# Three edits of an encoder kernel: where VectorE and GpSimd add, where the meta column is summed, and split weights kept in DRAM

## The chip, the cores and the metric

One Trainium2 chip, of which the kernel uses one core. A core has TensorE (PE, with its weight loads shown apart as PEld), VectorE (DVE), ScalarE (ACT), GpSimd (POOL) and SyncE (SP), which here issues every DMA. The metric is the device time of one execution, in microseconds; three runs of the kernel before are taken and their median counts. A further run is profiled.

## What is computed

One layer of a bidirectional encoder on two sequences with shared weights, one of 1024 tokens (s = 0, the long one) and one of 512 (s = 1, the sample). Sixteen meta tokens stand in front of each and are dropped at the end. Everything is float32.

```python
def mixer_sublayer(x, ...):
    n = rms_norm(x, g_mix)
    qa, ka, va, qb, kb, vb = jnp.split(n @ w_in, cuts, axis=-1)
    ...
    return x + concat(oa, ob) @ w_out

def conv_glu_sublayer(x, ...):
    n = rms_norm(x, g_ffn)
    gate = n @ w_ff_gate
    pad = jnp.pad(gate, ((0, 0), (1, 1), (0, 0)))
    gate = pad[:, :-2] * conv_w[0] + pad[:, 1:-1] * conv_w[1] + pad[:, 2:] * conv_w[2] + conv_b
    return x + (gelu(gate) * (n @ w_ff_up)) @ w_ff_down
```

After it comes a last RMSNorm. The model width is 1024, the feed-forward width 2816 (22 tiles of 128). The convolution looks one token to each side, so the first real token needs the gate of the last meta token: this one extra column is the meta column of the text.

## The kernel before

**Float32 products.** Activations lie with the features on the partitions and the tokens along the free dimension. Each operand of a product is split into a rounded part and a rest: `split` (L101) copies to `hi` on ACT (L104) and subtracts to `lo` on DVE (L105). `mm3` (L108) then multiplies three times, hi by hi, hi by lo and lo by hi (L110 to L112), into one PSUM sum. So each weight tile costs an ACT copy and a DVE subtraction before PE may use it. `split_half` (L129) splits 512 columns into one of five `w_hi` and one of five `w_lo` buffers (HB = 5).

**Order.** The program is scheduled as a whole ahead of the run: a scheduler orders the instructions of each engine by program order and its own idea of when they are ready. On the chip each engine then goes through its list in order, SP too, so an instruction that waits holds up all behind it on its engine.

**Stages.** The projections and attentions of both sequences come first and fill more than half of the time. The sample's `mixer_out` (L524, from about 519 us) runs beside the long sequence's attention; it loads each w_out tile, splits it and uses it (`load_weight`, L149, with three buffers each). The sample's `conv_glu` follows. The part that the change touches is mainly what comes after the long attention:

- `mixer_out_long` (L566, about 1345 to 1487 us) computes x + mix @ w_out for the long sequence in three parts of the tokens (PARTS). For each part it goes over the eight w_out tiles j anew: `load_halves` (L142) loads the tile and splits both halves, 24 matmuls follow, DVE adds the residual (L652), SP stores the sum `h`, and ACT and POOL sum squares. When a part is done, `combine` (L580) normalises it and splits the combinations that the next stage multiplies; it is a generator whose steps are taken between the tiles of the next part.
- `conv_glu_long` (L830, about 1487 to 2002 us) goes over eleven pairs of feed-forward tiles. A pair takes two fast products in Winograd's form (`winograd`, L785), one for the gate and one for w_up: seven products of half-size blocks instead of eight. Within one, the weight sums s1 to s4 are made on POOL (L794), the products land in one of eight PSUM buffers, and the sums of products are formed in `u` and `v` (ACT copies at L812 and L816, additions through L807 on DVE and, for `v`, on POOL). The meta column is a product with one column: ACT scales the raw weights by the column (L860), DVE reduces over the eight blocks (L862), PE sums over the partitions with a matrix of ones (L864), and ACT puts the result into the gate (L865). Then follow the convolution (L871 on ACT, L872 and L874 on DVE) and the GELU (L876). For w_up, DVE adds the product to the rest (L884) and POOL multiplies it by the gate's GELU (L885). POOL forms the activation differences for the down product (L893), and SP stores all seven operands in DRAM.
- The down product (from L904, about 2002 to 2258 us) is again such a fast product, seven products q = 0 to 6 over eleven steps f; the last one is cut in two halves. Here the weights' blocks a11 to a22 are loaded once and kept, `operand` (L938) forms the sums on POOL in place, `split_act` splits the activations, which are loaded for each product, and after each product four PSUM tiles are added to `u`, `v`, `c11`, `c22` on DVE (L997). The residual is added by POOL (L967). `norm` writes the output.

`load` (L919) keeps its DMAs in one fixed order. All of them stand on SP's queue.

## Time and profile before

| What | us |
|---|---|
| median of three runs | 2265.46 (2263.97 to 2266.13) |
| profiled execution | 2260.37 |
| its span, first to last instruction | 2258.6 |

The mean granted clock of TensorE is 0.963 of full speed. In the profile, a group of instructions is a line of the kernel, an engine, an operation and the tiles out<-in with their shape; then the count, the busy time in us, the mean of one in ns, and the idle time of that engine just before them with what ended most of it. Buffer numbers are left out of names, so `w_f` stands for `w_f` and `w_f2`. A table by windows gives, for each stretch, the busy time of each engine with the count of its instructions, the granted clock, the busy share of the 16 DMA engines and what they moved. Matmuls overlap each other, so the duration of one is longer than the step from one to the next.

### The profile page before, as it was taken

To read this page: it belongs to the slowest core of one execution; us is meant where nothing else is said; L and a number is where in the kernel's file an instruction comes from. 1 tells how busy PE (TensorE), PEld (TensorE's weight loads), DVE (VectorE), ACT (ScalarE), POOL (GpSimd) and SP (SyncE) were. 2 spreads that over 40 slices of the span, in tenths; PEclk is the share of its full clock that TensorE was granted. 3 is DMA by queue.
4 is the path that set the end of the run, shared out by engine and by line. 5 is a ranking of instruction groups with operands and counts; after the bars stand their busy time and mean duration, and the time that the engine had idled before them with its cause. 6 is when DMAs were issued, how large, how long until landed. Compare 5 with 4: busy or idle time off the path is not lost.

```text
span 2258.6 us, 35389 instructions
## 1 busy us (share of the span) xinstructions
PE 2075.1 (92%) x12186; PEld 1838.7 (81%) x12186; DVE 1708.6 (76%) x3599; ACT 1229.1 (54%) x2325; POOL 1140.6 (50%) x832
## 2 busy tenths in 40 slices
PE   7898998997999999999998999678999899998897
PEld 6898888996978998998998989676777777776677
DVE  6877787758788678888879766797767776747796
ACT  6534566635566565677667655455434444434354
POOL 3466456764454333455444313245566557526852
PEclk8999999998999999999999999888999999999999
DMA  6555334446312222232332237622222222265234
GB/s 222 165 183 184 114 108 145 157 167 195 101 59 66 96 71 75 81 113 90 104 101 72 75 102 212 175 74 87 93 84 103 80 84 101 86 212 184 80 119 134
DMA packets 156452, 268.52 MB, mean 119 GB/s; under 512 B 19792, under 2 KB 88944, under 8 KB 155760
## 3 DMA queue, kind: packets, MB, share of 16 engines
q1 hardware_dynamic: 156272, 266.26, 36.6%
q8 instruction: 96, 1.57, 0.3%
q14 instruction: 84, 0.69, 0.1%
HBM read 193.31 MB, written 72.88 MB: 118 GB/s over the span
## 4 chain that ended last, share of the span: by engine, by line
PE 53%; DVE 20%; issue 8%; POOL 7%; ACT 6%; DMA 5%; SPq 1%; POOLq 0%; DVEq 0%; ACTq 0%
PE ps_mm L111 12%; PE ps_mm L110 12%; PE ps_mm L112 12%; DVE w_lo L105 5%; PE ps_t L398 5%; PE ps_s L375 3%; PE ps_s L376 3%; DVE p L377 2%; DVE acc L862 2%; ACT w_hi L104 1%; PE ps_o L413 1%; PE ps_o L412 1%; DMA w_f<-w_out 1%; POOL act L885 1%; DVE act L872 1%
## 5 line engine op out<-in xcount | busy, mean ns | idle before, releaser
L110 PE MATMUL ps_mm<-xhi,w_hi 128*128 128x258 f32 (+3 forms) x1264 | 389.3, 308 | 12.1 <-ACT xhi L205 7.1
L111 PE MATMUL ps_mm<-xlo,w_hi 128*128 128x258 f32 (+3 forms) x1264 | 382.1, 302 | 9.2 <-DVE xlo L105 4.3
L112 PE MATMUL ps_mm<-xhi,w_lo 128*128 128x258 f32 (+3 forms) x1264 | 380.4, 301 | 0.0
L105 DVE TENSOR_TENSOR w_lo<-w_f,w_hi 128x512 fp32r<-128x512 f32 (+1 forms) x216 | 275.4, 1286 | 92.4 <-ACT w_hi L104 91.9
L377 DVE TENSOR_SCALAR_CACHE_REDUCE p<-ps_s 114x344 f32<-114x344 f32 (+4 forms) x562 | 257.7, 487 | 38.8 <-PE ps_s L376 20.8
L382 ACT ACTIVATE p<-p,nm 114x1040 f32<-114x1040 f32 (+5 forms) x212 | 215.0, 1014 | 87.3 <-DVE nm L380 83.9
L110 PEld LDWEIGHTS ps_mm<-xhi,w_hi 128*128 128x128 f32 x1264 | 241.6, 191 | 18.9 <-ACT xhi L205 8.0
L111 PEld LDWEIGHTS ps_mm<-xlo,w_hi 128*128 128x128 f32 x1264 | 241.9, 191 | 15.0 <-DVE xlo L105 5.4
L449 POOL TENSOR_TENSOR p<-p,r 128x1040 f32<-128x1040 f32 (+1 forms) x96 | 159.2, 1665 | 185.0 <-DVE r L384 115.8
L104 ACT CAST pt_hi<-ps_t 128x512 fp32r<-128x512 f32 (+6 forms) x360 | 168.4, 482 | 147.3 <-PE ps_t L398 127.0
L104 ACT CAST w_hi<-w_f 128x512 fp32r<-128x512 f32 (+1 forms) x233 | 187.0, 818 | 103.2 <-PE ps_mm L111 50.9
L112 PEld LDWEIGHTS ps_mm<-xhi,w_lo 128*128 128x128 f32 x1264 | 241.6, 191 | 0.9
L105 DVE TENSOR_TENSOR pt_lo<-ps_t,pt_hi 128x512 fp32r<-128x512 f32 (+4 forms) x312 | 171.9, 561 | 46.6 <-ACT pt_hi L104 45.2
L375 PE MATMUL ps_s<-k,q 128*114 128x348 f32 (+4 forms) x552 | 183.9, 338 | 14.5 <-DVE p L377 13.8
L398 PE MATMUL ps_t<-ident,p 128*128 128x128 f32 (+7 forms) x1188 | 184.1, 271 | 3.3 <-DVE pt_lo L105 2.1
L104 ACT CAST w_hi<-w_s 128x512 fp32r<-128x512 f32 x114 | 70.5, 619 | 208.3 <-PE ps_mm L111 113.1
L471 POOL TENSOR_TENSOR p<-p,c 114x1040 f32<-114x1040 f32 (+2 forms) x56 | 92.2, 1646 | 178.5 <-DVE c L469 111.4
L376 PE MATMUL ps_s<-k,q 128*114 128x348 f32 (+4 forms) x552 | 172.6, 317 | 0.4 <-DMA q<-qk 0.4
L398 PEld LDWEIGHTS ps_t<-ident,p 128*128 128x128 f32 (+7 forms) x1188 | 141.2, 136 | 33.2 <-issue 6.6
L110 PE MATMUL ps_s<-xhi,w_hi 128*128 128x256 f32 (+4 forms) x480 | 147.4, 312 | 10.6 <-ACT xhi L205 7.9
L112 PE MATMUL ps_s<-xhi,w_lo 128*128 128x256 f32 (+4 forms) x480 | 146.9, 307 | 4.4 <-DVE w_lo L105 4.3
L111 PE MATMUL ps_s<-xlo,w_hi 128*128 128x256 f32 (+4 forms) x480 | 147.2, 308 | 1.1 <-DVE xlo L105 1.0
(257 smaller groups left out, 5851.5 us busy)
## 6 DMA issues: line engine op xcount, KB each, us to landing
w_f<-w_gate SPq DMA_DIRECT2D x44, 512.0 KB, 3.3
w_f<-w_up SPq DMA_DIRECT2D x44, 512.0 KB, 3.3
w_f<-w_in SPq DMA_DIRECT2D x36, 512.0 KB, 4.0
w_f<-w_out SPq DMA_DIRECT2D x32, 512.0 KB, 4.2
a_f<-act SPq DMA_DIRECT2D x64, 256.0 KB, 2.7
w_f<-w_down SPq DMA_DIRECT2D x22, 512.0 KB, 3.3
act<-a_t SPq DMA_DIRECT2D x44, 256.0 KB, 2.0
a<-w_down SPq DMA_DIRECT2D x42, 256.0 KB, 3.8
```

The source lines that it names most:

```text
L104: nc.scalar.copy(hi, src)
L105: (lo_engine or nc.vector).tensor_tensor(out=lo, in0=src, in1=hi.bitcast(F32), op=ALU.subtract)
L110: nc.tensor.matmul(ps, lhsT=whi, rhs=xhi, start=start, stop=False)
L111: nc.tensor.matmul(ps, lhsT=whi, rhs=xlo, start=False, stop=False)
L112: nc.tensor.matmul(ps, lhsT=wlo, rhs=xhi, start=False, stop=stop)
L375: nc.tensor.matmul(ps, lhsT=q[0], rhs=k[:, c0:c0 + cw], start=True, stop=False)
L376: nc.tensor.matmul(ps, lhsT=q[1], rhs=k[:, c0:c0 + cw], start=False, stop=True)
L377: nc.vector.tensor_scalar(out=p[:, c0:c0 + cw], in0=ps, scalar1=HD ** -0.5, scalar2=-3.0e38, op0=ALU.mult, op1=ALU.max, accum_out=mx[:, i: ...
L382: nc.scalar.activation(p, p, AF.Exp, bias=nm, accum_out=l)
L398: nc.tensor.transpose(tps[:, c:c + M], p[:, k0:k0 + kw], g.ident[:M, :M])
L449: nc.gpsimd.tensor_tensor(out=p, in0=p, in1=r.broadcast_to([P, n]), op=ALU.mult)
L471: nc.gpsimd.tensor_tensor(out=p1, in0=p1, in1=c.broadcast_to([M, n]), op=ALU.mult)
```

## The change

There are three edits.

**VectorE in place of GpSimd.** In `winograd` the product p5 stays in PSUM and `v` is formed as p5 + u on DVE, where ACT had copied it and POOL had added. For w_up, DVE adds in PSUM and multiplies by the gate, where POOL had multiplied. In the down product the sums of weights move to DVE. Two of them are formed earlier: s2 during product 1 and a12 - a11 during product 2. For that, a21 is loaded for each step of product 0 and a22 for each step of product 1. The residual is loaded ahead into four buffers and added on DVE in PSUM; the one for `u` stays on POOL, after product 3.

**The meta column.** The scaled copies and the reductions are written at the head of a pair, before the gate's products; the matmuls with the ones stay behind these.

**Split parts in DRAM.** The sample's `mixer_out` stores the two parts of six w_out tiles (`PRE`), and `mixer_out_long` loads these parts, each in halves, where it had loaded and split the tile. Halves are now taken with the second one first.

```diff
...
 def load_halves(g, wp, src):
 
     w = load_whole(wp, g, src)
-    parts = [split_half(g, wp, w[:, i * H:(i + 1) * H]) for i in range(2)]
+    parts = [split_half(g, wp, w[:, i * H:(i + 1) * H]) for i in (1, 0)][::-1]
     return [p[0] for p in parts], [p[1] for p in parts]
+def load_parts(g, wp, src):
+    out = [None] * 2, [None] * 2
+    for i in (1, 0):
+        for part, tl, tag in zip(src, out, ("w_hi", "w_lo")):
+            tl[i] = wp.tile([P, H], F32R, name=tag, tag=tag, bufs=HB)
+            g.nc.sync.dma_start(out=tl[i].bitcast(F32), in_=part[:, i * H:(i + 1) * H])
+    return out
 
 
 def load_weight(g, wp, src, bufs=2, ahead=2, lo_engine=None):
...
                 split(g, xhi[k][:, c0:c0 + cw], xlo[k][:, c0:c0 + cw], m)
         for j in range(KT):
             w = load_weight(g, wp, g.w_out[j], bufs=wb)
+            if j in PRE:
+                for part, tl in zip(g.wo[j], w):
+                    nc.sync.dma_start(out=part, in_=tl.bitcast(F32))
             for c0, cw in chunks:
                 real = min(cw, C - 1 - c0)
                 res = mp.tile([P, cm], F32, name="res", tag="m")[:, :cw]
...
                 rows = g.oT[0][k * P:(k + 1) * P]
                 split(g, xhi[k], xlo[k], loaded("m", MB, rows[:, 1:], rows[:, 0:1]))
             for j in range(KT):
-                wj = load_halves(g, wp, g.w_out[j])
+                wj = load_parts(g, wp, g.wo[j]) if j in PRE else load_halves(g, wp, g.w_out[j])
                 rows = g.xT[0][j * P:(j + 1) * P]
                 res = loaded("res", 2, rows[:, NMETA:], rows[:, NMETA - 1:NMETA])
                 ps = g.psum.tile(P, cw, "s")
...
     def tile(tag):
         return up.tile([P, H], F32, name=tag, tag=tag, bufs=2)[:, :cw]
 
-    def add(engine, out, a, b):
-        engine.tensor_tensor(out=out, in0=a, in1=b, op=ALU.add)
+    def add(out, a, b):
+        nc.vector.tensor_tensor(out=out, in0=a, in1=b, op=ALU.add)
 
     s1 = s_(ALU.add, a21, a22)
     p1 = product(split_half(g, wp, a11), x["x11"])
...
     nc.scalar.copy(u, p1)
     yield 0, 0, product(split_half(g, wp, a12), x["x21"]), u
     p5 = product(split_half(g, wp, s1), x["t1"])
-    v = tile("v")
-    nc.scalar.copy(v, p5)
     s2 = s_(ALU.subtract, s1, a11)
     p6 = product(split_half(g, wp, s2), x["t2"])
-    add(nc.vector, u, p6, u)
-    add(nc.gpsimd, v, u, v)
+    add(u, p6, u)
+    v = tile("v")
+    add(v, p5, u)
     s3 = s_(ALU.subtract, a11, a21)
     p7 = product(split_half(g, wp, s3), x["t3"])
-    add(nc.vector, u, p7, u)
+    add(u, p7, u)
     yield 1, 1, p7, v
     s4 = s_(ALU.subtract, a12, s2)
     yield 0, 1, product(split_half(g, wp, s4), x["x22"]), v
...
     for f0 in range(0, NFF, 2):
         gate = up.tile([P, 2, N + 1], F32, name="gate", tag="gate", bufs=1)
         raw = [load_whole(wp, g, g.w_gate[f0 + i]) for i in range(2)]
+        first_sums = []
+        for i in range(2):
+            prod = up.tile([P, KT, P], F32, name="prod", tag="prod", bufs=1)
+            for k in range(KT):
+                nc.scalar.activation(prod[:, k], raw[i][:, k * P:(k + 1) * P], AF.Copy, scale=g.x0[:, k:k + 1])
+            acc = up.tile([P, P], F32, name="acc", tag="acc")
+            nc.vector.tensor_reduce(out=acc, in_=prod.rearrange("p k c -> p c k"), axis=AX.X, op=ALU.add)
+            first_sums.append(acc)
 
         for c0, cw in ((0, first), (first, H - first)) if f0 == 0 else ((0, H),):
             for i, half, ps, rest in winograd(g, wp, up, x, raw, c0, cw):
...
             es_h.close()
             ap = pool(es, g, "fa0", 1, "left")
         act = ap.tile([P, 2, N], F32, name="act", tag="act", bufs=2)
         for i in range(2):
-            prod = ap.tile([P, KT, P], F32, name="prod", tag="prod")
-            for k in range(KT):
-                nc.scalar.activation(prod[:, k], raw[i][:, k * P:(k + 1) * P], AF.Copy, scale=g.x0[:, k:k + 1])
-            acc = ap.tile([P, P], F32, name="acc", tag="acc")
-            nc.vector.tensor_reduce(out=acc, in_=prod.rearrange("p k c -> p c k"), axis=AX.X, op=ALU.add)
             ps = g.psum.tile(P, 2, "mm")
-            nc.tensor.matmul(ps, lhsT=acc, rhs=g.ones_d[:, 0:2], start=True, stop=True)
+            nc.tensor.matmul(ps, lhsT=first_sums[i], rhs=g.ones_d[:, 0:2], start=True, stop=True)
             nc.scalar.activation(gate[:, i, 0:1], ps[:, 0:1], AF.Copy, scale=float(D))
         for i in range(2):
             f = f0 + i
...
         raw = [load_whole(up, g, g.w_up[f0 + i], "w_f2") for i in range(2)]
         for i, half, ps, rest in winograd(g, wp, up, x, raw, 0, H):
             a = act[:, i, half * H:(half + 1) * H]
-            t = ap.tile([P, H], F32, name="sum", tag="sum", bufs=2)
-            nc.vector.tensor_tensor(out=t, in0=ps, in1=rest, op=ALU.add)
-            nc.gpsimd.tensor_tensor(out=a, in0=t, in1=a, op=ALU.mult)
+            nc.vector.tensor_tensor(out=ps, in0=ps, in1=rest, op=ALU.add)
+            nc.vector.tensor_tensor(out=a, in0=ps, in1=a, op=ALU.mult)
         (x11, x12), (x21, x22) = [[act[:, i, half * H:(half + 1) * H] for half in range(2)] for i in range(2)]
 
         def kept_act(nm, src):
...
         return blocks[nm, f]
 
     def sum_(out, op_, a, b):
-        nc.gpsimd.tensor_tensor(out=out, in0=a, in1=b, op=op_)
+        nc.vector.tensor_tensor(out=out, in0=a, in1=b, op=op_)
         return out
 
     def stage():
...
     def operand(q, f):
         if q < 2:
             w = weight(("a11", "a12")[q], f)
-            if f % 2 == q:
-                weight("a21", f)
+            weight(("a21", "a22")[q], f)
+            if q == 1:
+                sum_(blocks["a11", f], ALU.subtract, sum_(stage(), ALU.add, blocks["a21", f], blocks["a22", f]),
+                     blocks["a11", f])
             return w
         a11, a12, a21, a22 = [weight(nm, f) for nm in ("a11", "a12", "a21", "a22")]
         if q == 2:
 
-            return sum_(a11, ALU.subtract, sum_(stage(), ALU.add, a21, a22), a11)
+            sum_(a12, ALU.subtract, a12, a11)
+            return a11
         if q == 3:
-            sum_(a12, ALU.subtract, a12, a11)
             return sum_(stage(), ALU.add, a21, a22)
         if q == 4:
 
...
 
     u, v, c11, c22 = [result(nm) for nm in ("u", "v", "c11", "c22")]
 
-    def residual(out, k0, half):
+    def residual(k0, half):
+        out = []
         for j in range(HT):
-            res = op.tile([P, H], F32, name="res", tag="res", bufs=2)
-            nc.sync.dma_start(out=res, in_=g.h[k0 + j, :, half * H:(half + 1) * H])
-            nc.gpsimd.tensor_tensor(out=out[:, j], in0=out[:, j], in1=res, op=ALU.add)
+            out.append(op.tile([P, H], F32, name="res", tag="res", bufs=4))
+            load(out[j], g.h[k0 + j, :, half * H:(half + 1) * H])
+        return out
 
     def square(src, cw):
         sq = op.tile([P, H], F32, name="sq", tag="sq", bufs=4)[:, :cw]
...
             if f == LAGF and waiting:
                 waiting()
                 waiting = None
+            if f == LAGF and q in (1, 3, 4, 5):
+                res = residual(*{1: (0, 0), 3: (HT, 0), 4: (HT, 1), 5: (0, 1)}[q])
         cc = slice(c0, c0 + cw)
         for j in range(HT):
+            def out(tl, rest):
+                plus(ps[j], ps[j], rest)
+                plus(tl, ps[j], res[j])
             if q == 0:
                 nc.scalar.copy(u[:, j], ps[j])
             elif q == 1:
-                plus(c11[:, j], ps[j], u[:, j])
+                out(c11[:, j], u[:, j])
             elif q == 3:
                 plus(v[:, j], ps[j], u[:, j])
+            elif q == 4:
+                plus(u[:, j], ps[j], u[:, j])
+                out(c22[:, j], v[:, j])
             elif q == 5:
-                plus(v[:, j], ps[j], v[:, j])
+                out(v[:, j], v[:, j])
             else:
-                if q == 4:
-                    plus(c22[:, j], ps[j], v[:, j])
                 plus(u[:, j, cc], ps[j], u[:, j, cc])
+            if q == 3:
+                nc.gpsimd.tensor_tensor(out=u[:, j], in0=u[:, j], in1=res[j], op=ALU.add)
         if q == 1:
-            residual(c11, 0, 0)
             squares(acc1, c11, True)
         elif q == 4:
-            residual(c22, HT, 1)
-            residual(v, 0, 1)
-            residual(u, HT, 0)
             squares(acc2, c22, True)
         elif q == 5:
             squares(acc2, v, False)
...
 K2 = 8
 MB = 3
 HB = 5
+PRE = (0, 1, 2, 4, 5, 6)
 SB = 2
 AT = 3
 AF_ = 4
...
+    g.wo = {j: dram.tile([2, P, D], F32, name=f"wo{j}") for j in PRE}
     g.act = dram.tile([NFF // 2, len(TS), P, H], F32, name="act0")
     nc.scalar.preload_act_table_set(EXP_LN)
     g.vec = const.tile([P, V_N], F32, name="vec")
```

## The prediction

> **What bounds the kernel now.** I read the page first, for the busy shares, then the clock of each stretch in a table by windows, then, stage by stage, the matmul groups with the idle time before them, and last the timeline around one such gap.
>
> ```profile
> span 2258.6 us, 35389 instructions
> PE 2075.1 (92%) x12186; PEld 1838.7 (81%) x12186; DVE 1708.6 (76%) x3599; ACT 1229.1 (54%) x2325; POOL 1140.6 (50%) x832
> ...
> PE 53%; DVE 20%; issue 8%; POOL 7%; ACT 6%; DMA 5%; SPq 1%; POOLq 0%; DVEq 0%; ACTq 0%
> ```
>
> PE is busy 92% of the span. So a change to the other engines pays only where PE stands still, or where its clock is reduced.
>
> ```profile
> 520.00:530.00 10.00, 4.85 (x18) 3.26 (x18) 5.26 (x18) 6.38 (x11) 4.52 (x4) 0.70 0.98 335
> 1360.00:1450.00 90.00, 80.70 (x495) 76.65 (x493) 62.35 (x116) 45.23 (x99) 30.07 (x32) 0.96 0.78 222
> 1440.00:1486.00 46.00, 28.38 (x162) 26.30 (x160) 37.51 (x57) 23.10 (x40) 8.80 (x8) 0.85 0.49 141
> 1486.00:1534.00 48.00, 32.78 (x173) 30.30 (x173) 42.98 (x55) 24.78 (x52) 20.68 (x14) 0.76 0.15 47
> 1574.00:1976.00 402.00, 374.18 (x1557) 300.43 (x1555) 288.78 (x292) 177.64 (x355) 249.55 (x163) 0.96 0.26 89
> 1706.00:1750.00 44.00, 41.52 (x181) 33.39 (x179) 31.74 (x33) 19.28 (x39) 27.43 (x19) 1.00 0.26 90
> 2002.00:2036.00 34.00, 29.10 (x117) 23.86 (x118) 14.88 (x22) 15.35 (x27) 0.23 (x1) 0.90 0.91 321
> 2067.00:2110.00 43.00, 29.92 (x103) 21.71 (x103) 28.84 (x23) 11.74 (x21) 43.00 (x29) 0.84 0.35 110
> ```
>
> Columns: stretch, length, busy time of PE, PEld, DVE, ACT, POOL, granted clock, DMA share, GB/s. The rows are: the sample's output projection starting; the long sequence's output projection (parts 0 and 1, then part 2); the first pair of feed-forward tiles; nine later pairs; one pair alone; the start of the down product; its third product. A stretch at clock c has lost (1 - c) of its length: 16.1 us in the 402.
>
> ```profile
> L582 PE MATMUL ps_s<-acc,ones_d 128*128 128x344 f32 (+1 forms) x4 | 3.0, 851 | 17.6 <-DVE h L652 12.3 <-POOL acc L515 5.3
> ```
>
> ```profile
> L864 PE MATMUL ps_mm<-ones_d,acc 128*128 128x2 f32 x3 | 1.0, 367 | 7.0 <-DVE acc L862 7.0
> ```
>
> ```profile
> L864 PE MATMUL ps_mm<-ones_d,acc 128*128 128x2 f32 x40 | 7.0, 245 | 27.9 <-DVE acc L862 27.9
> ```
>
> ```profile
> L111 PE MATMUL ps_mm<-w_lo,w_hi 128*128 128x512 f32 (+1 forms) x272 | 102.4, 398 | 1.3 <-DVE w_lo L105 1.3
> L110 PE MATMUL ps_mm<-w_hi 128*128 128x512 f32 (+1 forms) x272 | 102.0, 397 | 16.1 <-ACT w_hi L104 16.1
> L112 PE MATMUL ps_mm<-w_hi,w_lo 128*128 128x512 f32 (+1 forms) x272 | 75.1, 396 | 3.4 <-DVE w_lo L105 3.4
> ```
>
> These are PE's waits, in order of time: before the feed-forward, in its first pair, in the ten passes over L864 between 1574 and 1980, and in the down product. In the loop the meta column's product is the only group that waits notably. One pass shows why:
>
> ```profile
> 1707.54 0.68 DVE L847 TENSOR_TENSOR gate<-ps_mm,u 128x512 f32<-128x512 f32 x1
> 1707.92 0.16 ACT L865 ACTIVATE gate<-ps_mm 128x1 f32<-128x1 f32 x1
> 1708.14 1.88 DVE L862 TENSOR_REDUCE acc<-prod 128x128 f32<-128x1024 f32 x1
> ...
> 1710.07 0.38 PE L864 MATMUL ps_mm<-ones_d,acc 128*128 128x2 f32 x2 [2.48 <-DVE acc L862]
> ```
>
> The reduction for the second tile comes on DVE only behind the last gate addition, and PE, which runs in order, waits 2.48 us for it with the whole w_up product behind.
>
> **The change, part by part.** All sums are against the profiled execution: 2260.37 us, of which 2258.6 are span. The three timed runs have a median of 2265.46, 5.1 us more; I carry the difference over to it.
>
> *Meta column.* Its scaled copies (ACT) and reductions (DVE) are written at the head of a pair, in front of the gate products, and its matmuls stay behind them. The work is the same and only its place is new, so `acc` is ready long before L864. I count the 27.9 us of waiting as gone, and the 16.1 us at reduced clock with it, as in the pair 1706 to 1750 the clock was 1.00, and the others differ by a short half-speed stretch behind the gap. That is 44.0. What comes next is PE's own rate: (402 - 27.9 - 16.1) / 9.14 pairs of 44.0 = 39.2 us a pair. DVE has to keep up with that.
>
> ```profile
> L105 DVE TENSOR_TENSOR w_lo<-w_s,w_hi 128x512 fp32r<-128x512 f32 x74 | 68.0, 920 | 27.9 <-ACT w_hi L104 27.9
> L105 DVE TENSOR_TENSOR w_lo<-w_f,w_hi 128x512 fp32r<-128x512 f32 x54 | 63.1, 1190 | 20.5 <-ACT w_hi L104 20.5
> L862 DVE TENSOR_REDUCE acc<-prod 128x128 f32<-128x1024 f32 x19 | 36.7, 1933 | 0.0
> L872 DVE SCALAR_TENSOR_TENSOR act<-gate,vec,act 128x1024 f32<-128x1024 f32 x18 | 32.5, 1804 | 0.0
> L874 DVE SCALAR_TENSOR_TENSOR act<-gate,vec,act 128x1023 f32<-128x1023 f32 x18 | 31.1, 1729 | 0.3
> L807 DVE TENSOR_TENSOR u<-ps_mm,u 128x512 f32<-128x512 f32 x36 | 24.6, 685 | 21.3 <-POOL v L807 21.3
> ```
>
> ```profile
> L885 POOL TENSOR_TENSOR act<-sum,act 128x512 f32<-128x512 f32 x36 | 50.0, 1388 | 25.5 <-ACT act L876 12.9 <-DVE sum L884 12.6
> ```
>
> *Additions to DVE.* Per pair, two v additions and four multiplications move from POOL. Against 0.685 us for the row that reads PSUM and writes SBUF, that is 6 x 0.685 = 4.1 us more DVE work a pair; DVE has 288.78 x 44 / 402 = 31.6 now, so 35.7 of 39.2. No row shows DVE writing PSUM, as the new in-place sum does: its ends are 0.69 (the same row) and 1.78 (a DVE subtraction beside POOL, some 1.1 more); it may also save a little. I take the near row, as only the output's place differs. POOL loses 50.0 us of multiplying in the window. The split w_lo costs 0.92 to 1.19 here and 0.693 where POOL is idle (row below), so some of DVE's extra comes back. The wait of 21.3 us for POOL's v vanishes too. New: the multiplication now waits for the GELU on DVE, with the next w_lo splits and the additions that free PSUM behind it. Their cover is the five w_hi/w_lo buffers: a product uses one and takes 39.2 / 14 = 2.8 us, so four products, 11 us, are split ahead; PSUM has eight buffers. If the GELU comes later than that, PE waits instead. I give back 3 us of the 44: **-41**.
>
> *First pair.* L864's 7.0 us go; but 1486 to 1534 is DVE's (42.98 of 48), and 3.8 us of reductions now stand ahead of splits that PE needs. **-5** (between -15 with the lost clock, and +4).
>
> *Down product.* Weight sums go from POOL to DVE.
>
> ```profile
> 2098.58 0.62 ACT L104 CAST w_hi<-a 128x512 fp32r<-128x512 f32 x1 [8.84 <-POOL a L932]
> ```
>
> ```profile
> L932 POOL TENSOR_TENSOR w_s<-a,a 128x512 f32<-128x512 f32 x8 | 13.4, 1678 | 0.0
> L932 POOL TENSOR_TENSOR a<-w_s,a 128x512 f32<-128x512 f32 x8 | 11.0, 1384 | 0.0
> ```
>
> ```profile
> L105 DVE TENSOR_TENSOR w_lo<-a_f,w_hi 128x512 fp32r<-128x512 f32 x10 | 17.1, 1713 | 0.0
> ```
>
> ```profile
> L105 DVE TENSOR_TENSOR w_lo<-a_f,w_hi 128x512 fp32r<-128x512 f32 x11 | 7.6, 693 | 13.5 <-ACT w_hi L104 13.5
> ```
>
> ```profile
> 2006.90 0.79 PE L110 MATMUL ps_mm<-w_hi 128*128 128x512 f32 x1 [5.20 <-ACT w_hi L104]
> ```
>
> From 2067 to 2110 POOL is busy without a pause, the splits wait for it, and they cost 1.713 against 0.693 without POOL. Of PE's 16.1 + 1.3 + 3.4 = 20.8 us, 5.2 are the start (it waits for activations) and 2 I leave for other places; 13.6 go, with 43 x 0.16 = 6.9 of clock. An earlier last multiplication saves the start some 2. Against it: in the second product (11 steps of 12 matmuls, 31 us) DVE has 22 splits, 22 sums and 8 additions, 52 x 0.69 = 35.8, which spills into the third, where 33 splits and sums leave room; the residual's other additions fall into the fifth and sixth, with room as well; and the loads, moved forward, are 37 x 256 KB in that product, 313 GB/s, under the 321 that the start row shows. I give back 3: **-19** (-24 to -5).
>
> *Stored split parts.* Six of eight w_out tiles, three times, are loaded as 1 MB instead of 0.5 MB: 9.4 MB more, at 335 / 0.98 = 342 GB/s 27.6 us of DMA.
>
> ```profile
> L104 ACT CAST w_hi<-w_f 128x512 fp32r<-128x512 f32 x36 | 21.6, 613 | 15.4 <-DMA w_f<-w_out 13.9 <-PE ps_s L111 1.4
> ```
>
> In 1360 to 1450 there are 36 such casts, 18 tiles; three quarters, 13.5 tiles or 7.1 MB, ask for 20.7 us, and 0.22 x 90 = 19.8 us are free. So DMA is full there, and behind the longer loads on SP stand residuals, h stores and output stores. For it: ACT drops 16 us and DVE about as much, and part 2 (DVE 37.51 of 46, PE waiting 17.6 us at L582) is short of DVE. The twelve stores (6.3 MB, 18.8 us of DMA if all were exposed) hold three-deep buffers and stand on SP ahead of q loads; nobody waits for them for 750 us; 0. Ends for this part: -22 (L582 and clock gone) and +27.6. I take **+1**, near the middle, as full DMA and relieved engines about cancel.
>
> Sum: -41 - 5 - 19 + 1 = -64: 2196 profiled, **2201 us** against the median.
>
> ```profile
> a<-w_down SPq DMA_DIRECT2D x42, 256.0 KB, 3.8
> ```
>
> *Two rules of the Trainium skill.* A gap of 2.48 us costs clock (0.96 over the nine pairs, though 1.00 in one). The Trainium skill, "TensorE: Matmul & The Clock Gate", "What's actually happening", has the clock fall after an idle window of about 3.4 us; by it the short gaps would not lower the clock, and the sum would be -48. The parts come in loads of 256 KB, as w_down does here, and such loads made the 321 GB/s of the start row. The Trainium skill, "DMA: Bandwidth & Descriptors", "Measured", has 138 GB/s at 64 KB and 341 at 1 MB; at its lower figure 9.4 MB would take 68 us, an estimate, and the sum would be near 0. The start row, at 321, speaks against it.
>
> **The rivals.**
>
> 1. *DMA becomes the bound in the output projection*: all 27.6 us exposed, 2228. For: 0.78 busy already; against: a third of the loads falls where DMA is half idle.
> 2. *The wait moves inside the loop*: DVE stands for the GELU with splits behind, or the clock stays low; half the 41 returns, 2222. For: POOL waits 12.9 us for the GELU now.
> 3. *The short gaps aren't what lowers the clock*: 16.1 stay, 2217. It is the clock rule above, as a mechanism. Against: the pair at 1.00 and the fall only behind gaps.
> 4. *The change doesn't do what it says*: the reduction is still placed late on DVE; only the other parts remain, 2242. Against: its inputs are ready a pair early.
> 5. *Slower: DVE becomes the bound in the loop.* If every split took 1.713 beside POOL, a pair would cost 14 x 1.713 + 4 (reductions) + 7 (convolution, four passes) + 18 x 0.685 = 47.3, 3.3 over today's 44.0, times 11: +36; with -19 and +1, and nothing gained at the first pair, 2283. It decides from splits of 1.48 us (14 x 1.48 + 23.3 = 44); now their mean is 1.02, and POOL is to do less.
> 6. *Part 2's stall goes as well*: with the 17.6 us and 46 x 0.15 = 6.9 of clock less what DVE keeps, 22, in place of the +1: 2178.
>
> **How the numbers follow.** Forecast 0.50; rivals in order 0.14, 0.13, 0.04, 0.05, 0.03, 0.11. Faster by over 0.2% (4.5 us, about what a measurement tells): all but the fifth and a remainder: 0.95; within 0.02; slower 0.03. The range leaves out the fourth, the fifth and the ends of the first and sixth: 2174 to 2234.
>
> **What would show it.** Right: no wait before the ones matmul, clock 1.00 and some 39.5 us a pair in the loop; no POOL waits in the third down product; POOL far below 50%. Wrong: PE waiting for w_lo in the loop, DVE idle before the multiplication, DMA at 0.95 and PE waiting for weights between 1360 and 1450.

## The result and the profile after

The kernel after takes 2182.74 us (median of four runs, 2180.81 to 2183.69) against 2264.72 for the kernel before, a ratio of 0.9639 (95% interval 0.9622 to 0.9656): 82 us less. The prediction was 2201, 64 less. The profiled execution took 2180.81 us; its span:

```profile
span 2179.0 us, 35308 instructions
PE 2050.5 (94%) x12186; PEld 1823.4 (84%) x12186; DVE 1686.6 (77%) x3697; ACT 1197.2 (55%) x2265; POOL 933.7 (43%) x698
...
PE 63%; DVE 16%; DMA 6%; issue 6%; ACT 5%; POOL 3%; SPq 1%; POOLq 0%; DVEq 0%; ACTq 0%
```

POOL's share of the chain that ended last fell from 7% to 3%. To say where the 79.6 us between the two spans came from, one needs marks that both kernels have. Three serve: the residual additions of the long output projection, the GELU of each pair, and the end. These are the rows of single lines of the code, before and after (count, shortest/median/longest in ns, first and last start in us):

```profile
L652 DVE TENSOR_TENSOR h<-ps_s,res x24: 496/502/517, 1359.2 to 1484.2; 128x342 f32<-128x342 f32 x8, 128x344 f32<-128x344 f32 x8, 128x340 f32<-128x340 f32 x8
...
L876 ACT ACTIVATE act<-act x11: 1897/1901/1919, 1543.2 to 1982.4; 128x2048 f32<-128x2048 f32 x11
```

```profile
L665 DVE TENSOR_TENSOR h<-ps_s,res x24: 497/506/518, 1333.3 to 1472.3; 128x342 f32<-128x342 f32 x8, 128x344 f32<-128x344 f32 x8, 128x340 f32<-128x340 f32 x8
...
L891 ACT ACTIVATE act<-act x11: 1913/1917/1923, 1525.9 to 1928.2; 128x2048 f32<-128x2048 f32 x11
```

| Stage | before | after | difference | prediction |
|---|---|---|---|---|
| up to the last residual addition | 1484.2 | 1472.3 | -11.9 | +1 |
| from there to the first GELU | 59.0 | 53.6 | -5.4 | -5 |
| first to last GELU, ten pairs | 439.2 | 402.3 | -36.9 (-33.7 for 9.14 pairs) | -41 (for 9.14 pairs) |
| last GELU to the end | 276.2 | 250.8 | -25.4 | -19 |

The marks are set by DVE and ACT, so PE can be some matmuls further on at the same mark in one kernel than in another. The waits of PE in the loop, before and after, from 1574 to 1928 us (total, times, longest):

```profile
PE ps_mm L864 <- DVE acc L862: 22.9, 8, 4.0
```

```profile
PE ps_mm L112 <- DVE w_lo L105: 3.7, 6, 0.9
```

The wait for the meta column is gone and a small one for w_lo has come. The table by windows for the kernel after, with the columns of the prediction (length, PE, PEld, DVE, ACT, POOL, clock, DMA share, GB/s), shows the attention's end, the output projection, the loop, the second product of the down product, and all of it:

```profile
1250.00:1330.00 80.00, 79.07 (x536) 73.39 (x535) 56.96 (x137) 48.35 (x90) 23.03 (x12) 1.00 0.38 113
...
1360.00:1450.00 90.00, 78.27 (x470) 74.25 (x469) 50.70 (x95) 36.43 (x78) 25.26 (x31) 0.91 0.83 246
...
1574.00:1928.00 354.00, 350.33 (x1510) 280.71 (x1509) 294.44 (x333) 154.19 (x312) 161.88 (x106) 1.00 0.28 97
...
1983.00:2015.00 32.00, 32.00 (x143) 26.50 (x142) 31.96 (x55) 15.07 (x25) 0.00 (x0) 1.00 0.58 193
...
1949.00:2179.00 230.00, 215.55 (x1054) 181.53 (x1054) 181.75 (x286) 112.93 (x202) 26.93 (x20) 0.97 0.51 164
```

The clock in the loop is 1.00 (0.96 before). In the second product DVE is busy 31.96 of 32 us and PE 32.00 of 32: DVE is full there, and PE does not wait.

### The profile page after: what moved, and what is told of

The parts are those of the page before. It is cut to its first block, busy times and chain, and to the rows that moved or that the text cites. A ratio compares the mean times of both kernels' runs of the same rounds, so it can differ in the third digit from the quotient of the medians.

```text
span 2179.0 us, 35308 instructions
## 1 busy us (share of the span) xinstructions
PE 2050.5 (94%) x12186; PEld 1823.4 (84%) x12186; DVE 1686.6 (77%) x3697; ACT 1197.2 (55%) x2265; POOL 933.7 (43%) x698
## 4 chain that ended last, share of the span: by engine, by line
PE 63%; DVE 16%; DMA 6%; issue 6%; ACT 5%; POOL 3%; SPq 1%; POOLq 0%; DVEq 0%; ACTq 0%
PE ps_mm L110 15%; PE ps_mm L112 15%; PE ps_mm L111 15%; PE ps_t L408 4%; DVE w_lo L105 3%; PE ps_s L385 3%; DVE p L387 2%; PE ps_s L386 2%; DMA w_f<-w_in 2%; PE ps_o L423 1%; PE ps_o L422 1%; DMA yT<-y 1%; DMA m<-oT 1%; DVE acc L862 1%; ACT p L392 1%
## 5 line engine op out<-in xcount | busy, mean ns | idle before, releaser
L105 DVE TENSOR_TENSOR w_lo<-w_f,w_hi 128x1024 fp32r<-128x1024 f32 (+1 forms) x180 | 226.6, 1268 | 85.0 <-ACT w_hi L104 84.7
L104 ACT CAST w_hi<-w_f 128x1024 fp32r<-128x1024 f32 (+1 forms) x197 | 165.4, 855 | 63.3 <-PE ps_mm L111 34.0
```

The lines of the kernel that those rows point to most:

```text
L104: nc.scalar.copy(hi, src)
L105: (lo_engine or nc.vector).tensor_tensor(out=lo, in0=src, in1=hi.bitcast(F32), op=ALU.subtract)
```

## The experiments

All ratios are to the kernel before on the same chip, with 95% intervals; its medians there lie between 2264.16 and 2265.95. "Loop" is first to last GELU.

| Run | us | against before | ratio (interval) | loop |
|---|---|---|---|---|
| e1 meta column alone | 2246.61 | -18.3 | 0.9915 (0.9899 to 0.9932) | 422.5 |
| e4 additions of the loop alone | 2256.26 | -8.7 | 0.9959 (0.9946 to 0.9973) | 433.9 |
| e5 these two | 2221.46 | -42.7 | 0.9811 (0.9792 to 0.9830) | 399.7 |
| e3 down product alone | 2235.56 | -29.4 | 0.9874 (0.9856 to 0.9891) | |
| e2 stored parts alone | 2242.07 | -22.9 | 0.9901 (0.9884 to 0.9918) | 440.2 |
| e6 all but the parts | 2193.55 | -70.6 | 0.9685 (0.9667 to 0.9704) | |
| e12 parts in part 0 only | 2183.88 | -80.7 | 0.9638 (0.9622 to 0.9654) | |
| e7 all eight tiles | 2188.92 | -75.2 | 0.9665 (0.9644 to 0.9686) | |
| e9 tiles 0 to 3 | 2187.24 | -78.7 | 0.9644 (0.9626 to 0.9663) | |
| e10 tiles 4 to 7 | 2197.85 | -68.1 | 0.9698 (0.9683 to 0.9714) | |
| e8 multiplication on GpSimd | 2195.65 | -68.5 | 0.9695 (0.9675 to 0.9715) | 414.7 |
| e11 first pair's sums later | 2185.12 | -80.8 | 0.9639 (0.9623 to 0.9656) | |

### The loop: one edit does not pay without the other

e1 is the kernel before with only this part of the diff; e4 has only the hunks of `winograd` and of the w_up product; e5 has both.

```diff
         raw = [load_whole(wp, g, g.w_gate[f0 + i]) for i in range(2)]
+        first_sums = []
...
+            nc.vector.tensor_reduce(out=acc, in_=prod.rearrange("p k c -> p c k"), axis=AX.X, op=ALU.add)
+            first_sums.append(acc)
...
-            nc.tensor.matmul(ps, lhsT=acc, rhs=g.ones_d[:, 0:2], start=True, stop=True)
+            nc.tensor.matmul(ps, lhsT=first_sums[i], rhs=g.ones_d[:, 0:2], start=True, stop=True)
```

> The kernel before with the meta column's copies and reductions at the head of a pair, nothing else. Theory of the prediction (the short wait at the ones matmul also lowers the clock): the 27.9 us of waiting and the 16.1 us at reduced clock in the loop go, and the first pair's wait too; -38 to -47 us against before, granted clock 0.99 or more between the first pair and the last. Rival A (the short gaps are not what lowers the clock): -22 to -30, clock still 0.96. Rival B (without the additions on VectorE the wait goes to GpSimd's v and to its multiplication): less than -20, with a new wait for GpSimd in each pair.

```diff
-    add(nc.gpsimd, v, u, v)
+    add(v, p5, u)
...
-            nc.gpsimd.tensor_tensor(out=a, in0=t, in1=a, op=ALU.mult)
+            nc.vector.tensor_tensor(out=a, in0=ps, in1=a, op=ALU.mult)
```

> The kernel before with the additions of v and the multiplication by the gate on VectorE, nothing else; the meta column stays where it was. Theory: PE's wait at the ones matmul stays or grows, since two more additions of 0.7 us stand ahead of the last reduction on VectorE, and splits beside an idle GpSimd get shorter; between -6 and +8 us. Rival: what counted in the loop was GpSimd's occupation, which slows the splits and holds v; then -15 to -30 alone, and the wait at the ones matmul shrinks.

> The kernel before with the meta column early and the additions and the multiplication of the loop on VectorE; no stored parts, the old down product. Theory: the two edits need each other, since with the meta column alone PE came to wait for w_lo in 7 of 8 pairs (14.0 us in 354) and with both it waits 3.7; so -36 to -44 us against before, more than the sum of the two alone (-18.3 - 8.7 = -27), and the time from the second to the last GELU falls from 439 us to 402 to 406. Rival: the two add up, and what is missing came from the other edits; -24 to -30.

The meta column alone gives 18 us, not 40: rival B's size, though the engine that PE comes to wait for is another. The rows of the GELU in e1, e4 and e5:

```profile
L880 ACT ACTIVATE act<-act x11: 1912/1916/1923, 1546.7 to 1969.2; 128x2048 f32<-128x2048 f32 x11
```

```profile
L875 ACT ACTIVATE act<-act x11: 1902/1904/1919, 1543.0 to 1976.9; 128x2048 f32<-128x2048 f32 x11
```

```profile
L879 ACT ACTIVATE act<-act x11: 1917/1919/1922, 1547.8 to 1947.5; 128x2048 f32<-128x2048 f32 x11
```

Against 439.2, the loop loses 16.7 and 5.3 us by the single edits and 39.5 by both: 17.5 belong to the pair. So e4 lies just beyond its theory's -6, and e5 bears its theory out. PE's waits from 1574 to 1928 say why, e1, e4 and e5 in this order:

```profile
PE ps_mm L112 <- DVE w_lo L105: 14.0, 7, 2.7
```

```profile
PE ps_mm L863 <- DVE acc L861: 19.8, 8, 2.5
```

```profile
PE ps_mm L112 <- DVE w_lo L105: 2.5, 5, 0.7
```

With the column early and POOL still adding, the gap moves further down the pair: PE waits for a split that DVE reaches only behind the convolution and one of the moved reductions. With the additions on DVE and the column late, the old wait stays. Only with both is neither gap left.

e1 also shows what such a gap costs in clock. PE's timeline there, in start and duration:

```profile
1715.02 0.40 PE L111 MATMUL ps_mm<-x_lo,w_hi 128*128 128x512 f32 x1
1718.10 0.50 PE L112 MATMUL ps_mm<-x_hi,w_lo 128*128 128x512 f32 x1 [2.68 <-DVE w_lo L105]
...
1718.95 0.63 PE L112 MATMUL ps_mm<-x_hi,w_lo 128*128 128x512 f32 x1
1719.38 0.63 PE L110 MATMUL ps_mm<-x_hi,w_hi 128*128 128x512 f32 x1
...
1721.52 0.63 PE L112 MATMUL ps_mm<-x_hi,w_lo 128*128 128x512 f32 x1
1721.94 0.52 PE L110 MATMUL ps_mm<-t_hi,w_hi 128*128 128x512 f32 x1
...
1723.48 0.40 PE L110 MATMUL ps_mm<-t_hi,w_hi 128*128 128x512 f32 x1
1723.71 0.39 PE L111 MATMUL ps_mm<-t_lo,w_hi 128*128 128x512 f32 x1
```

Behind a gap of 2.68 us the step between matmuls is 0.43 us for some 3 us, then 0.23 again. The window idle for about 3.4 us that the Trainium skill, "TensorE: Matmul & The Clock Gate", "What's actually happening", asks for was not needed here.

Not every gap does this. Of the seven gaps in e1's loop, the four of 2.23 to 2.70 us have such a stretch behind them, the three of 1.17 to 1.40 us have none:

```profile
1846.60 0.50 PE L112 MATMUL ps_mm<-x_hi,w_lo 128*128 128x512 f32 x1 [1.40 <-DVE w_lo L105]
1846.94 0.39 PE L110 MATMUL ps_mm<-x_hi,w_hi 128*128 128x512 f32 x1
```

In the kernel before, six of the eight gaps from 1574 to 1928 are 2.47 to 2.49 us long (the others 4.0); four of these six have the stretch, and the two that end at 1710 and 1843 us have not. So the length alone doesn't decide it, and what does is not shown.

Which half of the additions matters is seen in e8, the kernel after with the w_up product's multiplication back on GpSimd:

```diff
-            nc.vector.tensor_tensor(out=ps, in0=ps, in1=rest, op=ALU.add)
-            nc.vector.tensor_tensor(out=a, in0=ps, in1=a, op=ALU.mult)
+            t = ap.tile([P, H], F32, name="sum", tag="sum", bufs=2)
+            nc.vector.tensor_tensor(out=t, in0=ps, in1=rest, op=ALU.add)
+            nc.gpsimd.tensor_tensor(out=a, in0=t, in1=a, op=ALU.mult)
```

> The kernel after, but the w_up product's sum goes to an SBUF tile and GpSimd multiplies it by the gate, as before; v stays on VectorE. Theory (the additions of v, at which VectorE stood for GpSimd, were what mattered, and the multiplication is only weight on GpSimd beside the splits): +2 to +8, 2185 to 2191. Rival (the multiplication is what mattered): +12 to +20. Rival (no matter): within 2, with some 3 us of VectorE's time a pair saved.

It costs 12.9 us against the kernel after (2195.65 against 2182.74): the theory fell. Of the 20.2 us of loop between e1 and the kernel after, the multiplication makes 12.4 (414.7 - 402.3), the larger half. DVE has four instructions a pair fewer, yet the splits of loaded tiles get longer, and PE's waits for w_lo in the loop go from 3.7 to 10.7 us. The group of these splits from 1574 to 1928, after and in e8, then the in-place sum and the multiplication on DVE after, then the sum of e8:

```profile
L105 DVE TENSOR_TENSOR w_lo<-w_f,w_hi 128x512 fp32r<-128x512 f32 x51 | 46.3, 921 | 24.0 <-ACT w_hi L104 24.0
```

```profile
L105 DVE TENSOR_TENSOR w_lo<-w_f,w_hi 128x512 fp32r<-128x512 f32 x52 | 69.7, 1366 | 0.2
```

```profile
L899 DVE TENSOR_TENSOR act<-ps_mm,act 128x512 f32<-128x512 f32 x35 | 23.8, 679 | 0.0
L898 DVE TENSOR_TENSOR ps_mm<-ps_mm,v 128x512 f32<-128x512 f32 x18 | 12.4, 690 | 0.0
```

```profile
L899 DVE TENSOR_TENSOR sum<-ps_mm,v 128x512 f32<-128x512 f32 x18 | 12.3, 681 | 0.0
```

A split reads two SBUF tiles, and that of a loaded tile goes from 0.921 to 1.366 us when POOL has more to do; that of a formed sum (w_s) hardly changes, 0.950 to 0.955. Operations with one operand in PSUM stay at 0.68 to 0.69. So an operation moved from POOL to DVE in PSUM costs DVE 0.68 and gives some of it back in the splits. The Trainium skill, "SBUF — State Buffer", "Who interferes with whom", says that a DVE instruction with two SBUF inputs contends with a GpSimd one that reads SBUF, and one with at most one SBUF input, outside the modes that use both ports, does not; these rows agree.

### The down product

e3 has the part of the diff from `sum_` to the end of the products, on the kernel before.

```diff
-        nc.gpsimd.tensor_tensor(out=out, in0=a, in1=b, op=op_)
+        nc.vector.tensor_tensor(out=out, in0=a, in1=b, op=op_)
...
-            residual(c11, 0, 0)
...
+                res = residual(*{1: (0, 0), 3: (HT, 0), 4: (HT, 1), 5: (0, 1)}[q])
```

> The kernel before with the down product's part alone: sums of weights on VectorE, two of them earlier, the residual loaded ahead and added on VectorE. Prediction: -19 for this part (-24 to -5), of which some 2 belong to the earlier start that the multiplication on VectorE gives, so -17 here. Theory from the traces: the down product is 23.2 us shorter after, all but 2 us of PE's waiting in it is gone, so -21 to -25. Rival: part of it comes from the loop's changes (activations ready earlier, a lighter GpSimd), and this run gives -12 or less.

29.4 us at the medians, more than the theory's 21 to 25; in the traces, one execution each, the time behind the last GELU falls by 24.5 (276.2 to 251.7), so not all of the 29.4 need lie in the down product. PE's waits in it before, and in e3:

```profile
PE ps_mm L110 <- ACT w_hi L104: 16.1, 4, 5.2
PE ps_mm L112 <- DVE w_lo L105: 3.4, 6, 1.1
PE ps_mm L111 <- DVE w_lo L105: 1.5, 6, 0.3
```

```profile
PE ps_mm L110 <- ACT w_hi L104: 5.3, 2, 5.1
PE ps_mm L112 <- DVE w_lo L105: 0.5, 1, 0.5
PE ps_mm L111 <- DVE w_lo L105: 0.4, 1, 0.4
```

21.0 us become 6.2, of which 5.1 are the start. The gain needs none of the loop's edits: the rival falls.

### The stored parts

e2 has them alone (the hunks of `load_halves`, `load_parts` and the two `mixer_out`) on the kernel before; e6 is the kernel after with `PRE = ()`; e7, e9 and e10 have other tiles in `PRE`: all eight, 0 to 3, 4 to 7.

> The kernel before with the stored parts of six w_out tiles and the order of the halves, nothing else. The prediction put this term at +1 (between -22 and +27.6). Theory formed from the two traces: the term was mis-sized; by the end of the long sequence's output projection the kernel after is 12.6 us ahead, and if the stored parts make that, this run is -10 to -16 us against before, with the wait of 17.6 us at the ones matmul of the combination down to about 8. Rival: the 12.6 us come of how the other edits move the order of the whole program (the schedule is made for all of it at once), and the parts alone give -4 to +4.

```diff
-PRE = (0, 1, 2, 4, 5, 6)
+PRE = ()
```

> The kernel after, but all eight w_out tiles are loaded and split three times as before, none is stored (the halves still come second half first). Theory: the stored parts are worth what they gave alone, so 2182.7 + 22 = 2200 to 2208 us, with the wait of 12 us before the first ones matmul of the combination back. Rival A: their worth depends on the other edits, and the time is 2190 to 2197. Rival B (the prediction's term, +1): 2179 to 2185.

The parts with the new order of the halves are worth 22.9 us on the kernel before, more than the 10 to 16 of the theory; the parts alone are worth 10.8 beside the other edits, order included (2193.55 - 2182.74). Both speak against the prediction's +1, and e6 lies where its rival A has it. The order of the halves doesn't make the 11.9 us up to the last residual addition: e6 has the new order, and that addition is at 1483.6, where before had 1484.2. But it may count behind it. From there to the first GELU e1, e3, e4 and e5, with the old order, take 57.8 to 60.2 us (before 59.0); e2 and e6, which have only the order in common, take 53.9 and 54.3. The two rows of e2:

```profile
L665 DVE TENSOR_TENSOR h<-ps_s,res x24: 499/507/517, 1333.5 to 1470.6; 128x342 f32<-128x342 f32 x8, 128x344 f32<-128x344 f32 x8, 128x340 f32<-128x340 f32 x8
...
L889 ACT ACTIVATE act<-act x11: 1898/1902/1918, 1524.5 to 1964.7; 128x2048 f32<-128x2048 f32 x11
```

No run has the order alone, so this stays a rival that is not tested.

> The kernel after with all eight w_out tiles stored as parts, not six. Theory (what counted was that ACT and DVE no longer split): -2 to -6 us, 2177 to 2181. Rival (DMA, at 0.83 of its time from 1360 to 1450 us, becomes the bound, as the prediction's first rival had it): two more tiles are 3.1 MB more over three passes, 9.2 us at 342 GB/s; +3 to +9, 2186 to 2192, with PE waiting for w_hi and w_lo from DRAM.

> The kernel after with w_out tiles 0 to 3 stored as parts, not 0, 1, 2, 4, 5, 6. Theory (the place counts: VectorE is late at the end of a part, where the combination's steps, the splits and the last residual additions meet, so only late tiles help): 2188 to 2194, with a wait of 8 to 13 us for h before the ones matmul of the combination back. Rival (the number counts, 12.1 us in the mixer over six tiles, 2 us each): 2185 to 2188, with that wait about 5.

> The kernel after with w_out tiles 4 to 7 stored as parts. Theory (the place counts): as fast as six or faster, 2177 to 2184, with 3.1 MB less to load in the three parts and no wait over 3 us for h. Rival (the number counts): 2185 to 2188.

All eight cost 6.2 us against six at the medians, though the intervals overlap. Two waits of e7 between 1330 and 1490, as against 1.2 and 1.3 us after:

```profile
PE ps_s L595 <- DVE h L665: 8.5, 1, 8.5
PE ps_s L110 <- DMA w_hi<-wo: 4.9, 4, 2.7
```

The waits for w_hi and w_lo from DRAM together are 6.1 us, against 3.7 after, and DMA is busy 0.90 of the time from 1360 to 1450, against 0.83. So the prediction's first rival, DMA as the bound, may begin here; the larger part is the wait for h, and what makes that is not shown.

The last four are no faster than none (2197.85 against 2193.55, the intervals overlap): from 1400 to 1450 DMA is busy 0.95 of the time, from 1330 to 1490 PE waits 6.1 us for w_hi and w_lo from DRAM, and the wait for h (12.2 us) is there all the same. So my theory that relief at the end of a part is what counts fell. The first four scatter from 2179.48 to 2196.20 and decide nothing by their time. That the start might count was read off the residual additions and the windows of e6 (first two fences) and e10, in which tile 0 isn't stored:

```profile
L665 DVE TENSOR_TENSOR h<-ps_s,res x24: 494/503/517, 1361.9 to 1483.6; 128x342 f32<-128x342 f32 x8, 128x344 f32<-128x344 f32 x8, 128x340 f32<-128x340 f32 x8
```

```profile
1250.00:1330.00 80.00, 74.73 (x498) 68.60 (x497) 61.96 (x141) 49.42 (x87) 24.41 (x13) 0.98 0.26 86
```

```profile
L665 DVE TENSOR_TENSOR h<-ps_s,res x24: 496/506/517, 1364.6 to 1488.5; 128x342 f32<-128x342 f32 x8, 128x344 f32<-128x344 f32 x8, 128x340 f32<-128x340 f32 x8
```

```profile
1250.00:1330.00 80.00, 74.46 (x492) 67.74 (x491) 63.63 (x140) 48.77 (x86) 25.55 (x14) 0.98 0.26 85
```

In both the first addition comes at 1362 to 1365 and PE is busy 74.5 to 74.7 of the 80 us before 1330; in the kernel after they are 1333.3 and 79.07. e12 tests it:

```diff
-                wj = load_parts(g, wp, g.wo[j]) if j in PRE else load_halves(g, wp, g.w_out[j])
+                wj = load_parts(g, wp, g.wo[j]) if j in PRE and o == 0 else load_halves(g, wp, g.w_out[j])
```

> The kernel after, but the six stored tiles are loaded as parts in the first of the three token parts only; parts 1 and 2 load and split whole tiles as before. Theory (what the stored parts bring lies at the start: with them the long output projection starts some 25 us earlier and fills PE from 1250 to 1330 us, 79 of 80 us busy against 75 without): PE again 79 of 80, and most of the 10.8 us that the parts are worth beside the other edits kept, 2182 to 2187, with 6.3 MB less to load. Rival (the relief of VectorE and ACT in parts 1 and 2 is what counts): 2189 to 2194, with a wait of some 12 us for h before the ones matmul of the combination.

```profile
1250.00:1330.00 80.00, 79.08 (x535) 73.41 (x534) 56.74 (x137) 47.98 (x88) 23.02 (x12) 1.00 0.38 113
```

With the parts used in the first part only, PE is as busy as with all (79.08), and the time is that of the kernel after (2183.88 against 2182.74, the intervals overlap). The wait for h is back at 12.0 us, and it hardly matters. So most of what pays comes with the first part. In the traces its first GELU stands 4.1 us behind that of the kernel after (1530.0 against 1525.9) and 7.9 ahead of that of e6 (1537.9).

An early start isn't enough, though. The profiled execution of e9, the slowest of its five (2196.20), starts early and has PE busy for 79.07 of the 80 us, yet ends its residual additions no earlier than e6, with a wait of 12.4 us for h:

```profile
L665 DVE TENSOR_TENSOR h<-ps_s,res x24: 493/510/517, 1340.6 to 1485.3; 128x342 f32<-128x342 f32 x8, 128x344 f32<-128x344 f32 x8, 128x340 f32<-128x340 f32 x8
```

### The first pair

```diff
+        def column_sums():
...
+        if f0:
+            column_sums()
...
             if f0 + c0 == 0:
                 drain(late)
+                column_sums()
```

> The kernel after, but in the first pair alone the meta column's copies and reductions stand behind the first piece of the gate products (the other ten pairs as in the kernel after). Theory (the prediction's first-pair term gave something back because two reductions, 3.9 us, stand ahead of a split that PE waits 4.5 us for): -3 to -6 us, 2177 to 2180, and that wait goes. Rival (VectorE is full in the first pair, 42.0 of 43 us, so what is put off is waited for later, at the ones matmul or at a later split): within 2 of the kernel after.

The edit took the copies and reductions out of the head of the first pair and put them behind its first piece. It did not test its theory: on DVE the reductions stand where they were, one of them (1490.07, 1.90 us) right ahead of the split that PE waits 4.5 us for, as in the kernel after (1487.59, 1.91 us). The likely reason, not shown, is that the program's scheduler put them back there. The time is the same.

## Why the prediction was right, and where its sizes were off

The direction, the range and what carries most of the 82 us were right: the waits of the loop and of the down product. The sum fell 18 us short because of the stored parts (set at a loss of 1 us, where they gain 10.8 to 22.9) and the down product, less what the loop was set too high. The range held the result because its lower end allowed for rival 6, whose reason is not the one that the runs show.

**The loop (-41 for 9.14 pairs, measured -36.9 for ten, so -33.7).** The gap goes, the clock is 1.00, and the new wait for w_lo, which I had paid 3 us for, is 3.7 in 354. The price of the clock was too high. I took (1 - 0.96) x 402 = 16.1 us beside the 27.9 of waiting, so 39.2 us for PE's own pair. After, a pair takes 402.3 / 10 = 40.2, less 3.7 / 354 x 40.2 = 0.4 of waiting: 39.8. By that the lost clock was 402 - 27.9 - 9.14 x 39.8 = 10 us, not 16. The trace of before gives nearly the same directly: from 1574 to 1976, 62 steps between matmuls take some 0.43 us in place of 0.23, which is 12 us. That the share of 0.04 counts the gaps too would explain the rest; it is not shown. The prediction put the whole sum under the meta column, and there it failed: e1 and e5 show that 17.5 of it exist only with the additions on DVE, which the text had counted as a cost to the pair and a wait for v that vanishes.

**The additions on DVE.** The near row was right: 0.690 for the sum in PSUM, 0.679 for the multiplication. DVE did not become the bound (rival 5): 294.4 of 354 us.

**The first pair (-5, measured -5.4).** The agreement of the number is luck as far as the runs show. The 7.0 us at L864 do go, and the reductions do stand ahead of a split that PE waits for (6.6 us for w_lo after, 5.0 before), as the text feared. But e1 and e5, which have the column early, take 59.4 and 60.2 us from the last residual addition to the first GELU, no less than before (59.0), and e2, which leaves the column late, takes 53.9. PE is further on at the mark in e1 (220 matmuls in the stretch, 205 before), so the column isn't without worth; how much of the 5.4 is the column's and how much comes of the order of the halves stays open.

**The down product (-19, measured -25.4; e3 alone -29.4 at the medians).** Right in mechanism, too small in size. The start came 2.2 us earlier (2006.90 - 1982.4 before, 1950.50 - 1928.2 after), as put. Of the waits 14.8 went in e3 for my 13.6. Of clock 256 x 0.05 - 230 x 0.03 = 5.9 us went, for my 6.9, by the row for all of the down product before, below, and that of after above. The 3 us that I gave back for the second product were not needed: DVE is full there and PE does not wait, nor for the loads that were moved forward. That makes 22.9 of the 25.4; what is left is about what two-digit clocks leave open. The window before, and the start after:

```profile
2002.00:2258.00 256.00, 224.21 (x1054) 183.11 (x1054) 192.72 (x219) 111.18 (x202) 132.34 (x88) 0.95 0.47 153
```

```profile
1950.50 0.80 PE L110 MATMUL ps_mm<-w_hi 128*128 128x512 f32 x1 [5.42 <-ACT w_hi L104]
```

**The stored parts (+1, measured -11.9 in their stage).** This term had the wrong sign, and by a way that was not on the list. I set full DMA against relief of ACT and DVE between 1360 and 1486. A good part of the gain lies before: PE waited in sum 13.0 us from 1150 to 1340 before and 4.8 after, and was busy for 79.07 of the 80 us from 1250, where the kernel before has this:

```profile
1250.00:1330.00 80.00, 74.85 (x505) 69.14 (x505) 62.34 (x138) 49.86 (x88) 23.42 (x13) 0.98 0.26 86
```

The two largest waits before, and their successors after:

```profile
PE ps_o L410 <- DVE pt_lo L105: 5.4, 2, 2.9
PE ps_mm L110 <- DVE gate L706: 3.7, 2, 1.9
```

```profile
PE ps_s L385 <- DVE p L387: 2.4, 4, 1.6
PE ps_mm L110 <- DVE gate L719: 1.1, 1, 1.1
```

Loads of parts need neither ACT nor DVE, and in every kernel that stores the first tiles the first residual addition of the long projection comes 19 to 28 us earlier than before, so PE has its matmuls beside what is left of the sample's feed-forward. That the ahead-made order makes this, rather than the loads alone, is argued; shown are the start and the busy time. The 11.9 is known to some 3 us: e1, e3, e4 and e5, which leave this stage's code as it was, end it between 1480.9 and 1487.6 (before 1484.2). Rival 6 came near the total (2178) from a stall whose going is not the main cause, as e12 has the stall and nearly the time. Rival 1 was wrong for six tiles; whether it begins with eight is open. Rival 4's 2242 keeps the first pair's -5, which hangs on the same reduction; without it the rival is 2247.

**What stays open.** Why e2 gives 22.9 us and the parts in company 10.8. The interval of e2 (0.0017 of 2265, 3.9 us to each side) takes up a part of the difference. In the traces the two are 18.0 us (2258.6 - 2240.6) and 12.9 (2191.9 - 2179.0), so only 5.1 apart, and the order of the halves, which e2 adds and e6 has already, may be that much: e6 is 5.3 us ahead of before at the first GELU (1537.9 against 1543.2). Nor is it settled why the 12.0 us of stall in e12 cost so little, and why e9's early start brought nothing in its profiled execution. Stage figures rest on one execution of each kernel; that of before, at 2260.37, lies 4.6 us under its median in the runs beside e1 to e4 (2264.95), so they come out that much smaller than differences of medians.

No run beat the kernel after by more than the intervals. e12 is as fast with a third of the part loads.

## What to carry to other kernels

A gap of an in-order engine is gone only when the next instruction that comes late is gone too; where two edits close successive gaps, each alone can show less than its share (16.7 and 5.3 us here, 39.5 together), so try them together before dropping one. Where DVE's operations on two SBUF tiles get longer while GpSimd works, moving GpSimd's work to DVE with an operand in PSUM can cost less than it seems. A resource freed in one stage can pay in the stage before, where an earlier start fills the idle time: look at when a stage begins, not only at what it waits for. And a stage total that agrees with the forecast proves nothing about its cause until a run has the edit alone.

## What was not expected of the hardware

The window of e1's loop:

```profile
1574.00:1928.00 354.00, 339.95 (x1438) 271.72 (x1437) 265.48 (x267) 160.19 (x330) 229.57 (x147) 0.98 0.26 91
```

Gaps of 2.2 to 2.7 us still cost clock: 0.98 over the stretch in e1, with steps of 0.43 in place of 0.23 us for some 3 us behind four of its seven gaps. The three up to 1.4 us cost none, nor did those of up to 0.9 after (1.00); between 1.4 and 2.2 no gap of these loops lies. And loads of 256 KB moved 343 GB/s in the first product after, with DMA busy 0.97 of the time; the prediction had held the loads moved forward against 321, from the start row of before:

```profile
1949.00:1983.00 34.00, 32.50 (x131) 26.70 (x132) 23.55 (x38) 17.48 (x30) 0.00 (x0) 0.90 0.97 343
```
